# A hybrid decoder block on one core: the local half gated straight from PSUM during the latent steps

## The chip, the core and the metric

The kernel runs on one core of a Trainium2 chip. The core has five engines, each with an instruction queue of its own: PE (TensorE, matrix products into PSUM), DVE (VectorE), ACT (ScalarE), POOL (GpSimd) and SP (SyncE, which here issues DMAs). Each queue is worked off in order; semaphores tie the queues together. The metric is the device time of one execution in microseconds; the median of three runs is compared.

## What is computed

One block of a decoder for 1024 tokens of width 1024, in fp32: two kinds of attention side by side, each with its own output product and its own sigmoid gate, then an output product, a residual and a gated FFN.

```python
h    = rmsnorm(x, mix_norm_g)
qa, ka, va, q_lat, kv_lat, k_r, g_a, g_b = split(h @ w_in)
o_a  = swa_sink_attention(rope(qa), rope(ka), va, sinks)      # local: 8 heads of 64, window 128
o_b  = mla_attention(...)                                    # latent: 8 heads, causal over all 1024
y    = sigmoid(g_a) * (o_a @ w_o_swa) + sigmoid(g_b) * (o_b @ w_o_mla)
x    = x + y @ w_out
h    = rmsnorm(x, ffn_norm_g)
x    = x + (silu(h @ w_gate) * (h @ w_up)) @ w_down          # D_FF = 2816
return rmsnorm(x, final_norm_g)
```

What is below called the local half is `sigmoid(g_a) * (o_a @ w_o_swa)`.

## The kernel before

**Products.** Each operand is split into a high and a low part by `split` (line 160: ACT copies the high part, L163, DVE subtracts it from the source to get the low part, L166), and `mm3` (lines 172 to 174) makes three matmuls of them. One matmul has 512 columns; its output stands in a PSUM bank. The large products, the output product and the FFN go by a scheme with seven products instead of eight (`Seven`, `xo`), which needs sums and differences of operand blocks; additions and subtractions stand in the helpers `add` (L180) and `sub` (L177), which are given the engine to use.

**Stages**, in the profile's time: projections and the gate product (to 345 us), which leaves the gates' pre-activations `g_a` and `g_b` in DRAM as 16 tiles `gate_d[0..15]` of 128 columns of y by 1024 tokens, and the local attention; latent q, k and v (to 379); the latent steps (379 to 564); `mix_b` (564 to 608); the output product `xo` (608 to 690), which ends with the second RMSNorm; the FFN (690 to 1113) and its down product.

**The latent steps.** 64 steps t, 8 heads of 8 query blocks. A step issues the score matmuls of step t+2 (L1245 to 1247), then transposes its own probabilities `p` (L1272). For each block of scores DVE adds the mask and reduces (L1255, result `nmb`), ACT takes the exponential (L1256), POOL inverts the row sum and scales (L1257, 1258), PE transposes into `pTb`, and ACT and DVE split the transposed block (`pth`, `ptl`). PE has room between these for other products: the table `fill` puts a half of a local product `mix_a(dc, sh, c0, n)` into some of the steps. `dc` is one of 8 column blocks of y, `sh` a half of the tokens; each pair (dc, sh) has one PSUM tile `oA`, which is complete after the second half. `mix_a` then copies oA into SBUF by ACT (L1351), and for dc ≥ 4 stores the result `ar` to DRAM. Thirteen of the 16 are in steps, three at or after the last step.

**mix_b.** For the 8 column blocks in the order `DCS = (0, 1, 4, 5, 2, 3, 6, 7)`, `load_sigs` loads the two gate tiles (and `ar` where it was stored), `sigmoids` applies the sigmoid on ACT (L1328, one 128x1024 instruction a tile) and multiplies `ar` by the first gate on POOL (L1526, two halves). `mix_b` makes the latent product `oB`, multiplies it by the second gate on DVE out of PSUM (L1503), and adds or subtracts the two halves; the result y then stands where the first gate was (`ya`). Sums of y's row blocks, which the output product needs, are made by DMAs that accumulate (`left_sum`, issued by POOL): by the table `SUMS` five inside mix_b, and eleven after it.

**The sums of w_out.** `out_sums(i)` makes sums of blocks of w_out in DRAM, in seven parts. Part 0 (two copies of 1 MB on SP's queue) is issued in the second step of the local attention, the parts 1 to 6 in the latent steps 40 to 58 by `OUT_AT`.

**The end of the output product.** `xo(q, b)` makes product q for row block b and adds it into `x2` or subtracts it (DVE, out of PSUM). `norm_a(b)` squares on ACT and gets ms and rstd on POOL (L360, L363); `norm_b(b)` scales on DVE (L1742); `to_h` transposes into the FFN's operand (L1575). From here to the FFN's 15th product PE, DVE, ACT and POOL follow the order in which the code is written (`manual_schedule`). Into it are put the loads of the first FFN weights (`ffn.load_part`, L1619) and the sums of their blocks (`ffn.mix(0)`, six POOL instructions, L180 and L177).

**The FFN.** For 11 block pairs j the gate and up products run through `Seven.run` (`fa`, `fb` in PSUM; `wl` the split weights; `pu` a partial result). `wd_out(j)` loads two tiles of w_down, makes four differences on POOL (L177, `wd`), and stores them for the down product: for j = 0 and 1 in their own blocks, where it follows product 5; for the rest after product 2 of their block; the last one too in block 3.

Of the kernel before, what the change touches and what calls it, by code (L numbers as in the profile page):

```python
# [89 lines left out]
def hybrid_block_kernel(  # L90
# [989 lines left out]
    for it in range(N_SW):  # L1080
# [6 lines left out]
        if it == 1:  # L1087
            out_sums(0)
# [238 lines left out]
    def sigmoid(i):  # L1327
        a = nc.scalar.activation(gate[i], gate[i], AF.Sigmoid)  # L1328
        if held[0]:
            tc.keep_in_program_order(a)  # L1330
# [4 lines left out]
    def mix_a(dc, sh, c0, n, ps=None):  # L1335
# [3 lines left out]
        if (sh, c0) == (0, 0):  # L1339
            if dc >= 4:  # L1340
                ar[dc] = U("ar")
# [8 lines left out]
        if c0 + n == 4:  # L1350
            nc.scalar.copy(ar[dc][:, half(sh)], oa_ps.pop((dc, sh)))  # L1351
            if sh == 1 and dc >= 4:
                nc.sync.dma_start(ar_d[dc - 4], ar.pop(dc))
# [16 lines left out]
    DCS = (0, 1, 4, 5, 2, 3, 6, 7)  # L1370

    def load_sigs(dc):
        for i in (dc, 8 + dc):
            load_sig(i)
# [42 lines left out]
    w_at = {t: u[0] // 2 for t, u in fill.items() if u[0] % 2 == 0 and u[1:] == (0, 0)}  # L1417
    pvq = []
    OUT_AT = {40: 1, 43: 2, 47: 3, 50: 4, 54: 5, 58: 6}
    for t in range(NT):  # L1420
# [25 lines left out]
        held[0] = True  # L1446
        if t == 3:
            load_oa(0, 1)
            load_oa(1, 1)
# [16 lines left out]
    if LATE:  # L1466
        mix_a(*rest.pop(0), 0, 4, PX("oA"))
    for _, hp, j in pvq:
        pv(hp, j)
    if not LATE:  # L1470
        mix_a(*rest.pop(0), 0, 4, PX("oA"))
# [7 lines left out]
    def mix_b(dc, i):  # L1479
# [3 lines left out]
        ga, gb = gate.pop(dc), gate.pop(8 + dc)  # L1483
        ya[dc] = ga

        def mixed(sh):
            cs = half(sh)
            if dc < 4:
                add(ga[:, cs], ga[:, cs], gb[:, cs], nc.vector)
            else:  # L1490
                nc.vector.scalar_tensor_tensor(ga[:, cs], ga[:, cs], -1.0, gb[:, cs], op0=ALU.mult, op1=ALU.subtract)

        def mixed_split(sh):
            cs = half(sh)
            if dc >= 4 or sh == 0:
                hi, lo = left[1 if dc < 4 else 2 if sh == 0 else 4]
                split(hi[:, dc % 4], lo[:, dc % 4], ga[:, cs])

        for sh in range(2):
# [3 lines left out]
            nc.vector.tensor_tensor(gb[:, cs], pb, gb[:, cs], op=ALU.mult)  # L1503
# [17 lines left out]
    def sigmoids(dc):  # L1521
        for i in (dc, 8 + dc):
            sigmoid(i)
        a_ = ar.pop(dc)
        for sh in range(2):
            nc.gpsimd.tensor_tensor(gate[dc][:, half(sh)], a_[:, half(sh)], gate[dc][:, half(sh)], op=ALU.mult)  # L1526

# [4 lines left out]
    sigmoids(DCS[0])  # L1532
# [3 lines left out]
    SUMS = {6: [(0, 0), (0, 1)], 7: [(0, 2), (1, 0), (1, 1)]}  # L1536
# [3 lines left out]
    for i, dc in enumerate(DCS):  # L1540
        if i in (1, 2):
            st.load_to(st.index[("ob", (1, 3)[i - 1])])
# [6 lines left out]
        if i + 1 < 8:  # L1549
            sigmoids(DCS[i + 1])  # L1550
        for n, k in SUMS.get(i, ()):
            left_sum(n, k)
        if i == 2:
# [3 lines left out]
        if i in (1, 3):  # L1557
# [529 lines left out]
```

## Time and profile before

| | us |
|---|---|
| runs | 1334.76, 1332.06, 1332.71 |
| median | 1332.71 |
| profiled execution | 1334.28 |
| its span | 1332.5 |

The median is what a later time is compared with; durations below come from the profiled execution, whose span is from the first instruction to the last. The clock that was granted to TensorE was 0.999 of full speed over the span.

How to read the rows shown in the prediction: a row of the timeline holds the start in us from the begin of the span, the duration in us, the engine, the line of the kernel, the operation, `out<-in`, the shapes, the count, and in brackets the idle time before it with what ended it. A row of the groups holds the count, then the busy time and the mean ns of one, then the idle time before them. An idle engine costs nothing unless another one waits for it.

### The profile page before, as it was taken

To read this page: it belongs to the slowest core of one execution; us is meant where nothing else is said; L and a number is where in the kernel's file an instruction comes from. 1 tells how busy PE (TensorE), PEld (TensorE's weight loads), DVE (VectorE), ACT (ScalarE), POOL (GpSimd) and SP (SyncE) were. 2 spreads that over 40 slices of the span, in tenths; PEclk is the share of its full clock that TensorE was granted. 3 is DMA by queue.
4 is the path that set the end of the run, shared out by engine and by line. 5 is a ranking of instruction groups with operands and counts; after the bars stand their busy time and mean duration, and the time that the engine had idled before them with its cause. 6 is when DMAs were issued, how large, how long until landed. Compare 5 with 4: busy or idle time off the path is not lost. (4 is left out here: it accounts for less than half of the span.)

```text
span 1332.5 us, 19056 instructions
## 1 busy us (share of the span) xinstructions
PE 1316.1 (99%) x6516; PEld 1105.5 (83%) x6516; DVE 923.7 (69%) x1493; ACT 644.4 (48%) x1306; POOL 592.7 (44%) x638
## 2 busy tenths in 40 slices
PE   9999999999999999999999999999999999999997
PEld 6899888888888888887887788888888888888886
DVE  7868677776767766698779766665665564663862
ACT  7434667665547666764555322323233222644452
POOL 2116546643324556354242765755676531022521
PEclk9999999999999999999999999999999999999999
DMA  9454532344476446879822354534543425996504
GB/s 375 156 185 156 170 116 84 100 135 171 169 227 184 96 111 143 271 298 244 240 109 101 142 189 166 207 136 171 182 167 141 167 100 194 365 379 241 174 17 141
DMA packets 89121, 237.26 MB, mean 178 GB/s; under 512 B 10049, under 2 KB 16705, under 8 KB 87873
## 3 DMA queue, kind: packets, MB, share of 16 engines
q1 hardware_dynamic: 84192, 225.29, 49.0%
q0 software_dynamic: 3392, 8.39, 3.5%
q10 hardware_dynamic: 1440, 2.36, 0.5%
q8 instruction: 52, 0.85, 0.3%
q14 instruction: 45, 0.36, 0.1%
HBM read 161.16 MB, written 78.51 MB: 180 GB/s over the span
## 5 line engine op out<-in xcount | busy, mean ns | idle before, releaser
L166 DVE TENSOR_TENSOR wl<-wr,wl 128x512 fp32r<-128x512 f32 x150 | 149.4, 1019 | 73.8 <-ACT wl L163 73.3
L166 DVE TENSOR_TENSOR lrv<-lr,lrv 128x1024 fp32r<-128x1024 f32 x77 | 105.1, 1396 | 50.2 <-ACT lrv L163 44.6
L163 ACT CAST lrv<-lr 128x1024 fp32r<-128x1024 f32 x77 | 80.1, 1052 | 95.0 <-PE fd L174 55.4
L172 PE MATMUL fd<-lrv 128*128 128x512 f32 x308 | 119.9, 389 | 0.0
L174 PE MATMUL fd<-lrv 128*128 128x512 f32 x308 | 119.8, 389 | 0.0
L173 PE MATMUL fd<-lrv 128*128 128x512 f32 x308 | 119.8, 389 | 0.0
L177 POOL TENSOR_TENSOR wr<-wr,sm 128x512 f32<-128x512 f32 (+1 forms) x38 | 45.7, 1211 | 147.9 <-DVE wl L166 129.6
L163 ACT CAST wl<-wr 128x512 fp32r<-128x512 f32 x150 | 87.3, 622 | 6.2 <-DVE t3l L177 2.8
L1257 POOL TENSOR_TENSOR denb<-denb,neg_one 128x1 f32<-128x1 f32 x64 | 40.8, 643 | 91.8 <-ACT p L1256 80.0
L166 DVE TENSOR_TENSOR wl<-sm,wl 128x512 fp32r<-128x512 f32 x60 | 51.7, 885 | 43.1 <-ACT wl L163 43.0
L173 PEld LDWEIGHTS fd<-lrv 128*128 128x128 f32 x308 | 57.8, 188 | 12.1
L172 PEld LDWEIGHTS fd<-lrv 128*128 128x128 f32 x308 | 57.8, 188 | 12.1
L174 PEld LDWEIGHTS fd<-lrv 128*128 128x128 f32 x308 | 57.8, 188 | 11.9
L1256 ACT ACTIVATE p<-scb,nmb 128x384 f32<-128x384 f32 (+3 forms) x64 | 47.8, 747 | 33.4 <-DVE nmb L1255 24.6
L166 DVE TENSOR_TENSOR ptl<-pTb,pth 128x512 fp32r<-128x512 f32 (+2 forms) x96 | 50.5, 552 | 16.8 <-ACT pth L163 16.5
L1255 DVE CUSTOM_DVE_ANT_0 scb<-scb,mask 128x384 f32<-128x384 f32 (+3 forms) x64 | 48.6, 761 | 15.3 <-PE scb L1247 14.3
L360 POOL TENSOR_SCALAR ms<-ss 128x1 f32<-128x1 f32 x32 | 9.1, 286 | 111.7 <-ACT x L465 36.5
L1630 ACT ACTIVATE act<-sm 128x512 f32<-128x512 f32 x11 | 7.0, 633 | 99.7 <-DVE sm L180 99.7
L1258 POOL TENSOR_SCALAR p<-p,denb 128x384 f32<-128x384 f32 (+3 forms) x64 | 48.2, 758 | 6.1
L1630 ACT ACTIVATE act<-pu 128x512 f32<-128x512 f32 x22 | 13.9, 632 | 74.7 <-DVE pu L180 74.7
L172 PE MATMUL fb<-t3h,wl 128*128 128x512 f32 x120 | 47.4, 395 | 1.1 <-DVE pu L180 1.1
L172 PE MATMUL fa<-t1h,wl 128*128 128x512 f32 x120 | 47.2, 393 | 1.2 <-ACT wl L163 1.2
(355 smaller groups left out, 4340.7 us busy)
## 6 DMA issues: line engine op xcount, KB each, us to landing
lr<-la_d SPq DMA_DIRECT2D x77, 256.0 KB, 5.3
wr<-in_w_gate_dram SPq DMA_DIRECT2D x22, 512.0 KB, 4.3
wr<-in_w_up_dram SPq DMA_DIRECT2D x22, 512.0 KB, 5.1
wd<-in_w_down_dram SPq DMA_DIRECT2D x22, 512.0 KB, 7.1
rb_d<-wd SPq DMA_DIRECT2D x22, 512.0 KB, 2.7
la_d<-sd SPq DMA_DIRECT2D x22, 512.0 KB, 5.1
lr<-rb_d SPq DMA_DIRECT2D x44, 256.0 KB, 5.4
lr<-in_w_down_dram SPq DMA_DIRECT2D x33, 256.0 KB, 5.2
```

What stands on the lines that cost most here:

```text
L163: i = nc.scalar.copy(hi, src)
L166: (eng or nc.vector).tensor_tensor(lo, src, hi.bitcast(F32), op=ALU.subtract)
L172: nc.tensor.matmul(ps, ah, bh, start=first and i == 0, stop=False, skip_group_check=go_on)
L173: nc.tensor.matmul(ps, ah, bl, start=False, stop=False, skip_group_check=go_on)
L174: nc.tensor.matmul(ps, al, bh, start=False, stop=last and i == n - 1, skip_group_check=go_on)
L177: eng.tensor_tensor(out, a, b, op=ALU.subtract)
L360: nc.gpsimd.tensor_scalar(ms, ss, 1.0 / width, EPS, op0=ALU.mult, op1=ALU.add)
L1255: nc.vector.tensor_tensor_reduce(s_, s_, m_, 1.0, -NEG, op0=ALU.add, op1=ALU.min, accum_out=nm)
L1256: nc.scalar.activation(p_, s_, AF.Exp, scale=-1.0, bias=nm, accum_out=den)
L1257: nc.gpsimd.tensor_tensor(den, den, neg_one[:, 0:1], op=ALU.pow)
L1258: nc.gpsimd.tensor_scalar(p[:, 0:w], p[:, 0:w], den, 0.0, op0=ALU.mult, op1=ALU.add)
L1630: nc.scalar.activation(dst, src, AF.Silu)
```

## The change

The logistic function is written as sigmoid(x) = (1 + tanh(x/2))/2. ACT makes the tanh (`twice_sigmoid`), the factor 1 is added where the gate is multiplied, and the factor 1/2 stands in the output product's residual additions. In `mix_a`, DVE multiplies oA by the gate straight out of PSUM, so the first eight gates are loaded and activated during the latent steps, and neither an ACT copy nor the POOL multiplication remains. mix_b goes through the columns in pairs (0, 4), (1, 5), ..., the row sums stand between them, and the weights of oB come a column earlier. Part 0 of `out_sums` is in latent step 34. `ffn.mix(0)` is split in two (`mix_of`), each after another norm, and `wd_out(0)` and `wd_out(1)` are in FFN blocks 4 and 5.

```diff
         sw[it].pop("norm")()
-        if it == 1:
-            out_sums(0)
...
-    def sigmoid(i):
-        a = nc.scalar.activation(gate[i], gate[i], AF.Sigmoid)
+    def twice_sigmoid(g):
+        a = nc.scalar.activation(g, g, AF.Tanh, scale=0.5)
...
             if dc >= 4:
-                ar[dc] = U("ar")
+                ar[dc] = gate[dc]
...
         if c0 + n == 4:
-            nc.scalar.copy(ar[dc][:, half(sh)], oa_ps.pop((dc, sh)))
-            if sh == 1 and dc >= 4:
-                nc.sync.dma_start(ar_d[dc - 4], ar.pop(dc))
+            nc.vector.scalar_tensor_tensor(ar[dc][:, half(sh)], gate[dc][:, half(sh)], 1.0, oa_ps.pop((dc, sh)),
+                                           op0=ALU.add, op1=ALU.mult)
+            if sh == 1:
+                gate.pop(dc)
+                if dc >= 4:
+                    nc.sync.dma_start(ar_d[dc - 4], ar.pop(dc))
...
-    DCS = (0, 1, 4, 5, 2, 3, 6, 7)
+    DCS = (0, 4, 1, 5, 2, 6, 3, 7)
     def load_sigs(dc):
-        for i in (dc, 8 + dc):
-            load_sig(i)
+        load_sig(8 + dc)
...
+    g_at = {a: fill[b][0] for a, b in zip([3] + slots, slots) if fill[b][1:] == (0, 0)}
+    g_at[NT - 3] = 3
-    OUT_AT = {40: 1, 43: 2, 47: 3, 50: 4, 54: 5, 58: 6}
+    OUT_AT = {34: 0, 40: 1, 43: 2, 47: 3, 50: 4, 54: 5, 58: 6}
...
         held[0] = True
+        if t in g_at:
+            load_sig(g_at[t])
+        if t in fill and fill[t][1:] == (0, 0):
+            twice_sigmoid(gate[fill[t][0]])
+        if t == NT - 1:
+            twice_sigmoid(gate[3])
...
-        ga, gb = gate.pop(dc), gate.pop(8 + dc)
-        ya[dc] = ga
+        ga, gb = ar.pop(dc), gate.pop(8 + dc)
+        ya[dc] = gb
...
-            nc.vector.tensor_tensor(gb[:, cs], pb, gb[:, cs], op=ALU.mult)
+            nc.vector.scalar_tensor_tensor(gb[:, cs], gb[:, cs], 1.0, pb, op0=ALU.add, op1=ALU.mult)
...
-    def sigmoids(dc):
-        for i in (dc, 8 + dc):
-            sigmoid(i)
-        a_ = ar.pop(dc)
-        for sh in range(2):
-            nc.gpsimd.tensor_tensor(gate[dc][:, half(sh)], a_[:, half(sh)], gate[dc][:, half(sh)], op=ALU.mult)
...
-    SUMS = {6: [(0, 0), (0, 1)], 7: [(0, 2), (1, 0), (1, 1)]}
+    SUMS = {2: [(0, 0)], 3: [(1, 0)], 4: [(0, 1), (2, 0)], 5: [(1, 1), (3, 0)], 6: [(0, 2), (2, 1)], 7: [(1, 2), (3, 1)]}
...
-        if i in (1, 2):
-            st.load_to(st.index[("ob", (1, 3)[i - 1])])
+        if i in (0, 1):
+            st.load_to(st.index[("ob", (1, 3)[i])])
...
-            sigmoids(DCS[i + 1])
+            twice_sigmoid(gate[8 + DCS[i + 1]])
...
-        if i in (1, 3):
-            st.conv_to(st.index[("ob", (1, 3)[i // 2])])
+        if i in (1, 2):
+            st.conv_to(st.index[("ob", (1, 3)[i - 1])])
...
-        if q in (1, 5, 7):
-            add(x_, ps, x_, nc.vector)
-        else:
-            sub(x_, x_, ps, nc.vector)
+        nc.vector.scalar_tensor_tensor(x_, ps, 0.5 if q in (1, 5, 7) else -0.5, x_, op0=ALU.mult, op1=ALU.add)
...
+    def mix_of(m):
+        a11, a21, a22 = ffn.part(0, m, 0, 0), ffn.part(0, m, 0, 1), ffn.part(0, m, 1, 1)
+        t = ffn.sums[(0, m)] = U("sm", F32, (P, 2, 4, P))
+        add(t[:, 0], a21, a22, nc.gpsimd)
+        sub(t[:, 1], t[:, 0], a11, nc.gpsimd)
+        sub(a21, a11, a21, nc.gpsimd)
...
-    for n, k in ((0, 3), (1, 2), (2, 0), (2, 1), (1, 3), (2, 2), (3, 0), (3, 1), (2, 3), (3, 2), (3, 3)):
+    for n, k in ((0, 3), (2, 2), (1, 3), (3, 2), (2, 3), (3, 3)):
...
     norm_a(1)
+    mix_of("g")
...
     norm_a(2)
+    mix_of("u")
...
     norm_a(3)
-    ffn.mix(0)
...
-        if (q, m) == (5 if j < 2 else 2, "u"):
-            if j < HF - 1:
-                wd_out(j)
+        if (q, m) == (2, "u") and 2 <= j < HF - 1:
+            wd_out(j)
+        if (q, m) == (4, "u") and j in (4, 5):
+            wd_out(j - 4)
```

`ffn.load_part(0, 0)` and `ffn.load_part(0, 1)` each stand one product of `xo` earlier than before.

Three places in the order of rows, where a row holds the line, the operation and `out<-in` with the tiles' names (the numbers behind names tell tiles of one kind apart). The first is on DVE, in latent steps around step 33, before and then after the change:

```order
L1255 ISA scb_5525,nmb_5532<-scb_5525,mask_4054 128x1024
L1255 ISA nmb_5532 128x1
L166 TENSOR_TENSOR ptl_5518<-pTb_5519,pth_5517 128x3x128
L1255 ISA scb_5553,nmb_5557<-scb_5553,mask_4054 128x128
L1255 ISA nmb_5557 128x1
L166 TENSOR_TENSOR ptl_5518<-pTb_5546,pth_5517 128x4x128
```

```order
L1253 ISA scb_5531,nmb_5538<-scb_5531,mask_4052 128x1024
L1253 ISA nmb_5538 128x1
L166 TENSOR_TENSOR ptl_5524<-pTb_5525,pth_5523 128x3x128
L1349 SCALAR_TENSOR_TENSOR sg_5425<-sg_5425,oA_5458 128x512
L1253 ISA scb_5559,nmb_5563<-scb_5559,mask_4052 128x128
L1253 ISA nmb_5563 128x1
L166 TENSOR_TENSOR ptl_5524<-pTb_5552,pth_5523 128x4x128
```

The product with oA (L1349) stands between a split and the next reduction (L1255 before, L1253 after). On ACT, at the same place, before and after:

```order
L163 CAST pth_5462<-pTb_5493 128x2x128
L1256 ACTIVATE p_5480,denb_5481<-scb_5475,nmb_5479 128x512
L1256 ACTIVATE p_5506,denb_5507<-scb_5498,nmb_5505 128x896
L163 CAST pth_5517<-pTb_5519 128x3x128
L1256 ACTIVATE p_5533,denb_5534<-scb_5525,nmb_5532 128x1024
L1351 COPY ar_5453<-oA_5452 128x512
L163 CAST pth_5517<-pTb_5546 128x4x128
```

```order
L163 CAST pth_5467<-pTb_5499 128x2x128
L1326 ACTIVATE sg_5425<-sg_5425 128x1024
L1254 ACTIVATE p_5486,denb_5487<-scb_5481,nmb_5485 128x512
L1254 ACTIVATE p_5512,denb_5513<-scb_5504,nmb_5511 128x896
L163 CAST pth_5523<-pTb_5525 128x3x128
L1254 ACTIVATE p_5539,denb_5540<-scb_5531,nmb_5538 128x1024
L163 CAST pth_5523<-pTb_5552 128x4x128
```

The copy of oA (L1351) is gone, and a tanh of a whole gate tile (L1326) stands ahead of two exponentials. The third place is on POOL, at the end of the output product: `ms` and `rstd` are those of norms 3 and 4 before, and of norms 1, 2 and 3 after:

```order
L360 TENSOR_SCALAR ms_7491<-ss_7489 128x1
L363 TENSOR_TENSOR rstd_7493<-ms_7491,neg_half 128x1
L180 TENSOR_TENSOR sm_7495<-wr_7348,wr_7377 128x512
L177 TENSOR_TENSOR sm_7495<-sm_7495,wr_7348 128x512
L177 TENSOR_TENSOR wr_7348<-wr_7348 128x4x128
L180 TENSOR_TENSOR sm_7499<-wr_7349,wr_7378 128x512
L177 TENSOR_TENSOR sm_7499<-sm_7499,wr_7349 128x512
L177 TENSOR_TENSOR wr_7349<-wr_7349 128x4x128
L360 TENSOR_SCALAR ms_7554<-ss_7552 128x1
L363 TENSOR_TENSOR rstd_7556<-ms_7554,neg_half 128x1
```

```order
L360 TENSOR_SCALAR ms_7355<-ss_7353 128x1
L363 TENSOR_TENSOR rstd_7357<-ms_7355,neg_half 128x1
L180 TENSOR_TENSOR sm_7359<-wr_7285,wr_7314 128x512
L177 TENSOR_TENSOR sm_7359<-sm_7359,wr_7285 128x512
L177 TENSOR_TENSOR wr_7285<-wr_7285 128x4x128
L360 TENSOR_SCALAR ms_7417<-ss_7415 128x1
L363 TENSOR_TENSOR rstd_7419<-ms_7417,neg_half 128x1
L180 TENSOR_TENSOR sm_7421<-wr_7286,wr_7315 128x512
L177 TENSOR_TENSOR sm_7421<-sm_7421,wr_7286 128x512
L177 TENSOR_TENSOR wr_7286<-wr_7286 128x4x128
L360 TENSOR_SCALAR ms_7479<-ss_7477 128x1
L363 TENSOR_TENSOR rstd_7481<-ms_7479,neg_half 128x1
```

The six instructions that stood in one block between norms 3 and 4 stand in two blocks of three, between norms 1 and 2 and between norms 2 and 3.

19 lines of the change are left out of this document (8 added, 11 removed).

## The prediction, made before the change had run

> **What bounds the kernel now.** I read the busy line first, then windows by stage, then what TensorE waited for, then the rows around each wait.
>
> ```profile
> PE 1316.1 (99%) x6516; PEld 1105.5 (83%) x6516; DVE 923.7 (69%) x1493; ACT 644.4 (48%) x1306; POOL 592.7 (44%) x638
> 379.00:564.00 185.00, 182.30 (x1147) 160.00 (x1146) 132.12 (x275) 127.38 (x289) 91.38 (x132) 1.00 0.59 164
> 564.00:608.00 44.00, 43.90 (x192) 35.46 (x191) 37.95 (x40) 28.58 (x34) 25.39 (x16) 1.00 0.78 287
> 608.00:690.00 82.00, 81.43 (x376) 66.57 (x375) 63.33 (x83) 39.43 (x65) 28.79 (x35) 1.00 0.72 203
> 690.00:751.00 61.00, 58.78 (x267) 47.49 (x265) 57.94 (x80) 31.18 (x58) 21.64 (x17) 1.00 0.33 119
> 751.00:1113.00 362.00, 361.85 (x1596) 299.66 (x1597) 226.67 (x268) 105.42 (x189) 219.13 (x152) 1.00 0.46 163
> ```
>
> A windows row holds the stretch, its length, the busy time of PE, PEld, DVE, ACT and POOL, the granted clock, the DMA share and GB/s. The five stretches are the latent steps, mix_b, the output product, the head of the FFN, and the rest of the FFN. TensorE is busy everywhere, so only its gaps can be won. The fourth stretch differs: DVE is at 57.94 of 61 us, so there DVE sets the pace. The waits of PE name the gaps, first from 564 to 760, then in the latent steps (engine and line, who was waited for, total, times, longest):
>
> ```profile
> PE fb L172 <- DVE pu L180: 1.1, 1, 1.1
> PE fa L172 <- ACT pu L861: 0.7, 1, 0.7
> PE tp L1575 <- DVE xn L1742: 0.5, 1, 0.5
> PE xo L172 <- ACT yh L163: 0.3, 1, 0.3
> PE xo L173 <- DVE wv L166: 0.2, 1, 0.2
> ...
> PE scb L1245 <- ACT p L1256: 1.1, 3, 0.6
> 700.87 0.39 PE L173 MATMUL fa<-b21l,wl 128*128 128x512 f32 x1
> 701.10 0.39 PE L174 MATMUL fa<-b21h,wl 128*128 128x512 f32 x1
> 702.22 0.50 PE L172 MATMUL fa<-b21h,wl 128*128 128x512 f32 x1 [0.73 <-ACT pu L861]
> ```
>
> The last three rows show what a gap costs. Matmuls of 512 columns start every 0.23 us (700.87, 701.10) and are drawn 0.39 long, so an idle of 0.73 is a start 1.12 after the last, 0.89 lost: every idle hides 0.16 more. The three gaps at the FFN's head, with that, lose 1.1+0.16, 0.7+0.16 (0.89) and 0.5+0.16: some 2.8 us.
>
> **The FFN's head: −2.8 us.** Two edits take POOL work away from it.
>
> ```profile
> 673.12 1.51 POOL L180 TENSOR_TENSOR sm<-wr,wr 128x512 f32<-128x512 f32 x1
> ...
> 682.91 0.19 POOL L360 TENSOR_SCALAR ms<-ss 128x1 f32<-128x1 f32 x1
> 678.56 0.19 ACT L1737 ACTIVATION_READ_ACCUMULATOR xn<-x 128x1 f32 x1
> 683.77 1.28 DVE L1742 SCALAR_TENSOR_TENSOR xn<-x,rstd,ffng 128x1024 f32<-128x1024 f32 x1 [1.49 <-POOL rstd L363]
> ```
>
> First, `ffn.mix(0)`, six operations from 673.12 until shortly before 682.91, stands on POOL ahead of the ms and rstd of norm 4. Its sum of squares was there at 678.75, but ms ran at 682.91, and DVE idled 1.49 us for it. DVE is the pacing engine here, so those 1.49 reach the next two gaps of PE, 0.66 and 0.89. Now three operations follow norm 1's rstd and three norm 2's; norm 4's rstd, done about 0.9 after its ms starts (682.91, and the waiting xn at 683.77), would come at about 679.7, before DVE is free (683.77 − 1.49 = 682.28). I take −1.5.
>
> ```profile
> 734.42 3.48 DVE L166 TENSOR_TENSOR wl<-wr,wl 128x512 fp32r<-128x512 f32 x2
> 735.61 1.74 POOL L177 TENSOR_TENSOR wd<-wd 128x512 f32<-128x512 f32 x1
> 741.23 1.77 DVE L166 TENSOR_TENSOR wl<-sm,wl 128x512 fp32r<-128x512 f32 x1
> 743.52 0.68 DVE L166 TENSOR_TENSOR wl<-sm,wl 128x512 fp32r<-128x512 f32 x1
> ```
>
> Second, `wd_out(0)` runs on POOL at 735 to 742. DVE subtractions beside it take 1.74 to 1.77 us, the same ones alone 0.68: three of them lose 2×1.06 + 1.09 = 3.2 us, and the gap of 1.26 that waits for DVE `pu` comes 8 us later. Without it I take −1.3. Together −2.8; bounds 0 (DVE stays late for its other 58 us of work) and −3.5 (smaller gaps go too). By the Trainium skill, "SBUF — State Buffer", Who interferes with whom, a DVE instruction with two SBUF inputs contends with a GpSimd one that reads SBUF, exclusively; by that rule, the trace agrees (1.77 against 0.68), and the whole 3.2 comes back.
>
> The two blocks go to FFN blocks 4 and 5. There nothing waits: PE 361.85 of 362 with DVE at 226.67 (63%) through all of the FFN blocks that hold the nine other calls, one of them two. Price 0; if the cover were gone, 3.2 us per call.
>
> **mix_b and the output product: −1.0 us.** POOL's 16 multiplications go, DVE's product with oB becomes one instruction that adds 1 and multiplies, and eleven row sums ahead of the output product become six, with ten instead of five inside mix_b.
>
> ```profile
> L1526 POOL TENSOR_TENSOR sg<-ar,sg 128x512 f32<-128x512 f32 x16 | 26.2, 1658 | 28.6 <-ACT sg L1328 28.6
> L1503 DVE TENSOR_TENSOR sg<-oB,sg 128x512 f32<-128x512 f32 x16 | 10.9, 681 | 2.5 <-ACT sg L1328 2.5
> L1189 DVE SCALAR_TENSOR_TENSOR qns<-q,qns 128x512 fp32r<-128x512 f32 x6 | 4.0, 686 | 3.2 <-ACT qns L1188 3.2
> L180 DVE TENSOR_TENSOR sg<-sg,sg 128x512 f32<-128x512 f32 x8 | 9.3, 1165 | 0.5
> ```
>
> The two-operation form with one PSUM input takes 686 ns against 681: 32 of them, in mix_b and the output product, cost 0.2 us of DVE, which had 6 and 19 us free. The eight additions L180 (1165 ns, beside those POOL rows) should near 0.7: DVE gains up to 3.9 us. So the output product's operand `yh` and the weights `wv` should be ready: their gaps, 0.3+0.16 and 0.2+0.16, are worth 0.8, and small ones make it 1.0. Bounds 0 and −1.5. The added sums are DMAs in the stretch with the highest share, 0.78; they leave the one after (0.72) by as many. The order in pairs (0, 4, 1, 5, ...) has every pair's rows complete two columns after they start, which is what lets a sum start at the third column; it adds no instruction, and the weights of oB are loaded and split one column earlier.
>
> **The latent steps: +0.5 us.** The 16 ACT copies of oA become DVE instructions, 13 of them inside the steps, and 8 tanh (half of the 16 gate activations, each of the same 128x1024) join ACT there.
>
> ```profile
> L1351 ACT COPY ar<-oA 128x512 f32<-128x512 f32 x16 | 9.3, 584 | 8.0 <-PE oA L174 7.9
> L1328 ACT ACTIVATE sg<-sg 128x1024 f32<-128x1024 f32 x16 | 16.3, 1053 | 0.0
> L1255 DVE CUSTOM_DVE_ANT_0 scb<-scb,mask 128x384 f32<-128x384 f32 (+3 forms) x64 | 48.6, 761 | 15.3 <-PE scb L1247 14.3
> ACT p L1256 <- DVE nmb L1255: 22.8, 26, 1.9
> 467.32 0.40 PE L174 MATMUL oA<-wv,wv 128*128 128x512 f32 x1
> 468.13 0.33 PE L1247 MATMUL scb<-kT,qT 96*128 96x384 f32 x1
> ```
>
> ACT: 8×1.05 − 13×0.584 = +0.8 us, and the 7.9 us in which it stood before a copy until oA was ready are gone, and nothing on ACT gets later by it. DVE: 13×0.69 = +9.0 us on 132 of 185, at the head of a queue whose next entry is mostly a score reduction. The chain that can hurt: the reduction gives `nmb`, ACT's exp waits for it (22.8 us in 26 waits), and PE waits for exp (1.1 in 3). But the reduction itself waits 14.3 us for PE's scores: DVE is ahead of PE. In the order of rows nearly every product with oA is followed by a reduction whose scores PE issues after that oA: here oA's last matmul starts at 467.32 and the last of the next scores at 468.13, 0.8 later, so 0.69 fits between them. Two of the 13 stand ahead of a split whose transposition PE ends first, and can hold it back by up to 0.7 each: 1.4 at most, with scores two steps ahead (a step is 185/64 = 2.9 us). On the other side PE's waits for exp, 1.1+3×0.16 = 1.6, may vanish because ACT no longer stands waiting for oA. New waits: a gate load is queued on SP behind the store of a product with oA (dc ≥ 4), which waits for DVE, and its tanh stands in ACT's order ahead of the next exps, which PE's transpositions wait for. Mostly three or four steps (9 to 12 us) lie between load and tanh, but from step 29 to 30 and from 57 to 58 one (2.9 us).
>
> ```profile
> oar<-oa_d SPq DMA_DIRECT2D x4, 512.0 KB, 5.6
> ```
>
> A load of that size in these steps lands after 5.6 us, so ACT may stand 5.6 − 2.9 = 2.7 us twice. The chain behind it (reduction 0.76, exp and POOL's two rows about as long each) fills some 3 of the 5.8 us of lead, so PE loses little of the 2.7: 0.25 a place. With the 1.4 set off against the 1.6 I take +0.5. Bounds +9.0 (all thirteen products exposed) and −1.6.
>
> A rule against this edit: the Trainium skill, "VectorE: DVE Perf Modes", Specifications, has VectorE sitting closer to SBUF and ScalarE closer to PSUM, so the evacuation moves to the engine that is worse at it. The rows agree as far as 584 against 686 ns go, and by them alone the move would cost 16×0.1 = 1.6 us of engine time, and the sum would be 1.6 higher if all of it were exposed.
>
> **The rest: 0.** `out_sums(0)` leaves its place at 154 us, on SP:
>
> ```profile
> 153.44 0.50 PE L172 MATMUL fa<-t1h,wl 128*128 128x512 f32 x1 [1.18 <-ACT wl L163]
> 154.27 1.23 SPq L337 DMA_DIRECT2D wt_d<-in_w_out_dram  x2
> ```
>
> The only wait that is listed for PE from 139 to 345 ends at 153.44, before those copies are issued; nothing there is won. At its new place, step 34, a further 2 MB on SP's queue lies in a stretch with a DMA share of 0.59; its first user is the sum at step 40, six steps later (6×2.9 = 17 us).
>
> Sum: −2.8 − 1.0 + 0.5 = −3.3. The profiled run took 1334.28, its span 1332.5, so the same run would take 1331.0. It lies 1.6 above the median of 1332.71; by the median 1329.4.
>
> **Rivals.**
>
> *DVE in the latent steps decides* (slower). DVE takes its rows in order, so each product with oA that waits for PE holds back the reduction and the transposition's split behind it. Place: the change's L1349 ahead of its L1253 (the reduction). With all 13 exposed 9.0 − 3.8 = +5.2: 1337.9. From 6 exposed the change no longer wins, from 10 it loses over 0.2%. For it: PE already waits for exp. Against: the reductions' 14.3 us of waiting. Chance 0.22.
>
> *The split mix holds up the norms* (same). Three operations stand ahead of norm 2's ms and may wait for weights.
>
> ```profile
> 655.10 0.48 SPq L1619 DMA_DIRECT2D wr<-in_w_up_dram  x1
> wr<-in_w_up_dram SPq DMA_DIRECT2D x22, 512.0 KB, 5.1
> 659.94 0.55 POOL L363 TENSOR_TENSOR rstd<-ms,neg_half 128x1 f32<-128x1 f32 x1
> 665.67 0.19 POOL L360 TENSOR_SCALAR ms<-ss 128x1 f32<-128x1 f32 x1 [5.19 <-ACT xn L1737]
> ```
>
> The gap from 660.5 to 665.67 is 5.2 and the operations take 4.9 (half of 673.12 to 682.91): it fits by 0.3, if weights are there. In the old place they land at 655.10+5.1 = 660.2, and one product earlier now. Late by 2 or 3 us, norm 2 and what follows it would give the head's 2.8 back: 1331.7; from 6.5 us on it turns slower than the 0.2% below. Chance 0.09.
>
> *The head stays DVE-bound* (same). With 57.94 of 61 us busy, each gap closed can open behind the next late row; only 1 us is kept over all: 1331.7. For it: DVE idles just 3 us there. Against: 4.7 us leave DVE's path. Chance 0.13.
>
> *The steps gain too.* ACT, rid of 7.9 us of waiting, brings exp forward, and of the lost time there 3 us go, twice the waits for exp: 1329.4 − 3.0 = 1326.4. For it: PE's first wait there is for ACT `p`. Against: most of the 2.7 us by which PE's 182.30 misses 185 has other causes. Chance 0.10.
>
> The forecast keeps 0.46. 0.2% is 2.7 us, about what a measurement of this kernel can tell from no change: faster means below 1330.0. The forecast lies 0.6 beyond that, and its own range is 1326.5 to 1331.5: 0.30 of its 0.46 go to faster, 0.16 to same. With the steps' gain, 0.10, and 0.06 of the two rivals that end near no change, faster is 0.46. Slower is 0.20: 0.17 of the first rival (10 and more exposed) and 0.03 of the split mix. Same is the rest, 0.34. The range runs from 1325.0 to 1336.5: the steps' gain at its low end, all but full exposure of the thirteen at its high one.
>
> **What would show it.** Right: in the new profile no PE wait for `xn`, `pu` at the head, norm 4's rstd not behind any POOL add, DVE rows of 0.7 where 1.7 stood at 734 to 742, L1349 at some 0.69 us with reductions still waiting for PE scores. Wrong: PE waits for `p` or `scb` in the latent steps above 2 us, exp waiting for `nmb` well over 22.8 us, or new waits on DVE at the head; then the forecast falls by that term.

## The result and the profile after

The changed kernel takes 1328.81 us (median of 6 runs, 1326.63 to 1329.56); the kernel before, on the same chip, 1333.03 (1332.06 to 1334.76). The ratio is 0.9962, with a 95% interval of 0.9952 to 0.9972: 5.1 us faster, between 3.7 and 6.4. It is not the ratio of the two medians, which lie 4.2 us apart. Forecast were 3.3 us faster and 1329.4.

The busy line of the page after the change, and two stretches of its windows view (stretch, length, busy time of PE, PEld, DVE, ACT, POOL, granted clock, DMA share, GB/s):

```profile
PE 1315.0 (99%) x6516; PEld 1107.4 (83%) x6516; DVE 916.1 (69%) x1509; ACT 635.8 (48%) x1289; POOL 563.6 (42%) x622
```

```profile
608.00:690.00 82.00, 82.00 (x384) 68.28 (x383) 62.00 (x80) 36.80 (x62) 21.04 (x27) 1.00 0.55 167
690.00:751.00 61.00, 61.00 (x281) 50.44 (x280) 55.33 (x79) 28.88 (x54) 22.06 (x17) 1.00 0.26 93
```

PE has no idle time left in the output product and at the FFN's head, where it was busy 81.43 of 82 and 58.78 of 61. The view of PE's waits from 564 to 760, which had five rows before, has none. Such windows are cut at fixed times, though; where a kernel starts later, its work lies elsewhere in them. So I measure the stages between the starts of their first matmuls, which the timeline gives, in us:

| kernel | to the first scores | latent steps | mix_b | output product | FFN | down product | span |
|---|---|---|---|---|---|---|---|
| before | 379.48 | 184.12 | 44.40 | 82.20 | 425.54 | 216.76 | 1332.5 |
| after | 378.95 | 185.23 | 43.52 | 80.48 | 422.14 | 216.66 | 1327.0 |

(The output product runs to its last matmul, the FFN from there to the first of the down product.) The terms of the change stand in the four columns in the middle: +1.1 in the latent steps, −0.9 in mix_b, −1.7 in the output product, −3.4 in the FFN, together −4.9, which agrees with the −5.1 of the runs. The first column differs by 0.5; it differs by up to 5 us between executions of kernels that are alike there (376.4 to 381.2 in the runs below), so it is start-up and no part of the change. Where the code of a stage is the same, the latent steps and mix_b repeat within 0.2 us and the FFN within 0.5; the output product of e1, with the code of before, took 0.5 more. So one profile can tell changes of 1 us apart which the runs, with an interval of some 1.3 us to each side, hardly do; a difference below 0.5 in the output product or the FFN counts only with a wait that shows it.

### The profile page after: what moved, and what is told of

It is laid out like the page before. It is cut to its first block, busy times and chain, and to the rows that moved or that the text cites. A ratio compares the mean times of both kernels' runs of the same rounds, so it can differ in the third digit from the quotient of the medians.

```text
span 1327.0 us, 19016 instructions
## 1 busy us (share of the span) xinstructions
PE 1315.0 (99%) x6516; PEld 1107.4 (83%) x6516; DVE 916.1 (69%) x1509; ACT 635.8 (48%) x1289; POOL 563.6 (42%) x622
## 4 chain that ended last, share of the span: by engine, by line
PE 62%; POOL 2%; issue 2%; DVE 1%; ACT 0%; POOLq 0%; DVEq 0%; ACTq 0%
PE fa L174 6%; PE fa L173 6%; PE fa L172 6%; PE fd L172 5%; PE fd L173 5%; PE fd L174 5%; PE fb L173 5%; PE fb L174 5%; PE fb L172 5%; PE xo L174 2%; PE xo L172 2%; PE xo L173 2%; POOL p L1256 1%; POOL denb L1255 1%; PE oB L173 1%
## 5 line engine op out<-in xcount | busy, mean ns | idle before, releaser
L166 DVE TENSOR_TENSOR wl<-wr,wl 128x512 fp32r<-128x512 f32 x150 | 144.3, 984 | 74.2 <-ACT wl L163 73.7
L1255 POOL TENSOR_TENSOR denb<-denb,neg_one 128x1 f32<-128x1 f32 x64 | 40.0, 624 | 92.5 <-ACT p L1254 80.5
L1253 DVE CUSTOM_DVE_ANT_0 scb<-scb,mask 128x384 f32<-128x384 f32 (+3 forms) x64 | 48.4, 760 | 17.1 <-PE scb L1245 15.6
L163 ACT CAST pth<-pTb 128x512 fp32r<-128x512 f32 (+2 forms) x96 | 43.4, 480 | 18.1 <-PE pTb L1270 17.2
L172 PE MATMUL fb<-t2h,wl 128*128 128x512 f32 x120 | 47.4, 395 | 0.0
```

Source lines behind the costliest of these rows:

```text
L163: i = nc.scalar.copy(hi, src)
L166: (eng or nc.vector).tensor_tensor(lo, src, hi.bitcast(F32), op=ALU.subtract)
L172: nc.tensor.matmul(ps, ah, bh, start=first and i == 0, stop=False, skip_group_check=go_on)
L1253: nc.vector.tensor_tensor_reduce(s_, s_, m_, 1.0, -NEG, op0=ALU.add, op1=ALU.min, accum_out=nm)
L1255: nc.gpsimd.tensor_tensor(den, den, neg_one[:, 0:1], op=ALU.pow)
```

## The experiments

Twelve kernels, all of them variants of before or after. The table holds the ratio to before with its interval (none for e6 and e7, which leave out a part of the computation and were timed only once) and the stages.

| run | edit | ratio | latent steps | mix_b | output product | FFN |
|---|---|---|---|---|---|---|
| e1 | before, `wd_out` moved | 0.9996 [0.9987, 1.0004] | 184.15 | 44.41 | 82.73 | 424.22 |
| e2 | before, mix split, loads earlier | 1.0014 [1.0005, 1.0024] | 184.15 | 44.42 | 86.49 | 424.23 |
| e3 | after, old list of sums | 0.9963 [0.9950, 0.9976] | 185.17 | 43.52 | 80.48 | 421.85 |
| e4 | after, `out_sums(0)` back | 0.9962 [0.9950, 0.9975] | 188.29 | 43.52 | 80.48 | 422.09 |
| e5 | after, second DVE instruction | 0.9981 [0.9971, 0.9992] | 188.73 | 43.52 | 80.45 | 421.84 |
| e6 | after, no tanh in the steps | – | 184.18 | 43.52 | 80.48 | 422.25 |
| e7 | after, ACT copies, no gating | – | 184.75 | 43.52 | 80.48 | 421.92 |
| e8 | after, sums held to the last tanh | 0.9960 [0.9946, 0.9974] | 185.25 | 43.52 | 80.48 | 421.91 |
| e9 | after, FFN's head as before | 0.9984 [0.9974, 0.9993] | 185.27 | 43.52 | 80.48 | 425.04 |
| e10 | after, sums held to mix_b's end | 0.9994 [0.9984, 1.0004] | 185.35 | 43.52 | 85.54 | 422.29 |
| b3 | after, tanh at short steps | 0.9964 [0.9952, 0.9977] | 185.12 | 43.52 | 80.48 | 421.91 |
| b4 | b3, weights split earlier | 0.9952 [0.9938, 0.9965] | 185.97 | 43.52 | 80.45 | 421.96 |

### The FFN's head: each edit alone, and both undone

e1 is the kernel before with one edit:

```diff
-        if (q, m) == (5 if j < 2 else 2, "u"):
-            if j < HF - 1:
-                wd_out(j)
+        if (q, m) == (2, "u") and 2 <= j < HF - 1:
+            wd_out(j)
+        if (q, m) == (4, "u") and j in (4, 5):
+            wd_out(j - 4)
```

> The kernel before with only wd_out(0) and wd_out(1) moved to FFN blocks 4 and 5. My theory: the subtractions on DVE at 734 to 742 us take 0.7 instead of 1.7 us, the wait of PE for pu at 749 us (1.1 idle, 1.28 lost) is gone, the other two gaps at the FFN's head stay: -1.3 us, and nothing is lost in blocks 4 and 5. Rival (the head stays DVE-bound): the gap reappears behind the next DVE row, 0 to -0.4 us.

PE's waits from 600 to 760 in e1:

```profile
PE fa L172 <- ACT pu L861: 0.7, 1, 0.7
PE tp L1575 <- DVE xn L1742: 0.5, 1, 0.5
PE xo L172 <- ACT yh L163: 0.5, 1, 0.5
PE xo L173 <- DVE wv L166: 0.2, 1, 0.2
```

The wait of `fb` for `pu` is gone and the other two of the head are there as before. e1's timelines of POOL and DVE show why; the first and the last of the DVE rows answer to 734.42 and 741.23 of before, the one between them to a row of 1.18 us at 738.42:

```profile
732.49 1.62 POOL L177 TENSOR_TENSOR wr<-wr,sm 128x512 f32<-128x512 f32 x1 [1.88 <-ACT act L1630]
732.88 2.38 DVE L166 TENSOR_TENSOR wl<-wr,wl 128x512 fp32r<-128x512 f32 x2
735.79 0.68 DVE L166 TENSOR_TENSOR wl<-wr,wl 128x512 fp32r<-128x512 f32 x1
736.99 0.68 DVE L166 TENSOR_TENSOR wl<-sm,wl 128x512 fp32r<-128x512 f32 x1
```

Of the pair only one subtraction got faster, 2.38 us for both instead of 3.48: the other stands beside a POOL row that isn't `wd_out`'s and stays. The next two went from 1.18 and 1.77 to 0.68, and the product `act` between them (L1632) from 1.78 to 0.68, 3.8 us in all. The FFN is 425.54 − 424.22 = 1.3 us shorter, blocks 4 and 5 included. The runs alone don't show it: the whole kernel is 0.5 us faster by the ratio, with an interval that holds nothing as well as the 0.8 by which the stages are shorter (the output product took 0.5 more here).

e2 is the kernel before with the other edit (the two loads also leave their old places, behind `norm_b(0)` and behind `norm_a(1)`; that is two products of `xo` earlier, not one as I wrote in the description of the change):

```diff
     ahead(4, 0)
+    ffn.load_part(0, 0)
     xo(3, 0)
...
     ahead(4, 1)
+    ffn.load_part(0, 1)
...
     norm_a(1)
+    mix_of("g")
...
     norm_a(2)
+    mix_of("u")
...
     norm_a(3)
-    ffn.mix(0)
```

> The kernel before with only ffn.mix(0) split in two behind norms 1 and 2, and its loads one product earlier. My theory: norm 4's DVE instruction no longer idles 1.49 us for rstd, the gaps of PE for xn and pu (0.64 and 0.89 lost) go: -1.5 us; the gap at 749 us stays. Rival (DVE-bound): 0 to -0.5. Rival (the split mix waits for weights and holds up norm 2): 0 to +2, with ms of norm 2 ended by a POOL add.

The FFN gained 1.3 us, as expected, but the output product lost 4.3, and the kernel is slower than before. e2's PE waits, then its timeline on POOL, SP and PE (the last row sum, the first FFN load, the gap), and the first two of these before the change:

```profile
PE xo L172 <- ACT yh L163: 2.2, 2, 2.0
PE fb L172 <- DVE pu L180: 1.1, 1, 1.1
PE tp L1575 <- DVE xn L1742: 0.8, 1, 0.8
PE fa L172 <- ACT pu L861: 0.3, 1, 0.3
PE xo L173 <- DVE wv L166: 0.2, 1, 0.2
```

```profile
641.67 0.88 POOL L328 DMA_DIRECT2D sg<-sg  x1 [1.84 <-DMA sg<-sg]
...
640.02 0.33 SPq L1619 DMA_DIRECT2D wr<-in_w_gate_dram  x1
...
650.57 0.50 PE L172 MATMUL xo<-wv,yh 128*128 128x512 f32 x1 [2.01 <-ACT yh L163]
```

```profile
643.71 0.88 POOL L328 DMA_DIRECT2D sg<-sg  x1 [1.86 <-DMA sg<-sg]
653.34 0.67 SPq L1619 DMA_DIRECT2D wr<-in_w_gate_dram  x1
```

Before, the FFN's first load was issued 10 us after the last row sum, because it stood behind the first store of x2; in e2 it is issued 1.7 us ahead of it. The last three row sums, with KB each and us from issue to landing, before (639 to 650 us) and in e2 (637 to 650), where the first FFN loads run beside them:

```profile
sg<-sg POOLq DMA_DIRECT2D x3, 256.0 KB, 4.1
```

```profile
sg<-sg POOLq DMA_DIRECT2D x3, 256.0 KB, 7.7
```

The sums land later, the split of `yh` behind them is late, and PE waits 2.0. No mix operation has run by then, so of the two parts of the edit it is the loads. The wait for `xn` in the list is not the one of the FFN's head, which is gone: it stands inside the output product, at 673.46, and what makes it these runs don't settle. Of the wait for `pu` at the head 0.3 of 0.7 is left. POOL's `ms` rows in e2 still wait for ACT, not for a mix operation (668.32, ended by ACT `xn`), so it isn't the wait for weights of my rival.

e9 undoes both edits in the changed kernel (the diffs of e1 and e2 the other way round).

> The changed kernel with the head of the FFN as before: ffn.mix(0) in one piece behind norm 3, the loads one product later, wd_out(0) and (1) in their own blocks. If the head's two edits gained 3.4 us there and need nothing else: the stretch from the last product of xo to the down product 425.5 us again, the output product 80.5: +3.4. If the gated local half alone made part of it (DVE less behind): +2.

```profile
PE fb L172 <- DVE pu L180: 1.1, 1, 1.1
PE fa L172 <- ACT pu L861: 0.7, 1, 0.7
```

Two of the three waits are back, and the FFN is 2.9 us longer; the third, for `xn`, isn't, so 0.5 us of the 3.4 came from the other parts of the change. The runs agree: 0.9984 against 0.9962 is 2.9 us. Together, then, the head's edits gain 2.9 where the row sums are early, and e1's and e2's gains in the FFN add up to 2.6.

### Where the output product's gain is from

In e3 the table of sums and the list behind mix_b are the old ones.

```diff
-    SUMS = {2: [(0, 0)], 3: [(1, 0)], 4: [(0, 1), (2, 0)], 5: [(1, 1), (3, 0)], 6: [(0, 2), (2, 1)], 7: [(1, 2), (3, 1)]}
+    SUMS = {6: [(0, 0), (0, 1)], 7: [(0, 2), (1, 0), (1, 1)]}
...
-    for n, k in ((0, 3), (2, 2), (1, 3), (3, 2), (2, 3), (3, 3)):
+    for n, k in ((0, 3), (1, 2), (2, 0), (2, 1), (1, 3), (2, 2), (3, 0), (3, 1), (2, 3), (3, 2), (3, 3)):
```

> The changed kernel with the row sums where they were: five inside mix_b, eleven after it. The trace of the change gained 0.9 us in mix_b and 1.7 in the output product, 2.6 where I had forecast 1.0. If the earlier sums are what made the output product's operands ready: +1.0 to +1.7 us in the output product, with PE waits for yh back. If it was the POOL multiplications that went: 0 to +0.3.

Nothing changed: 80.48. POOL has nothing but the sums to do in mix_b now, so a place further back in the code is no place further back in its queue; only the order among the sums differs. Before, the multiplications for the last column were ahead of the first sum. The first sum and the first matmul of the output product, of before and then of after, and after's last sum and first FFN load:

```profile
608.70 1.84 POOL L328 DMA_DIRECT2D sg<-sg  x2
608.00 0.39 PE L172 MATMUL xo<-wv,yh 128*128 128x512 f32 x1
```

```profile
578.41 0.94 POOL L328 DMA_DIRECT2D sg<-sg  x1 [24.30 <-DMA ffng<-in_ffn_g_dram]
607.70 0.39 PE L172 MATMUL xo<-wv,yh 128*128 128x512 f32 x1
627.32 0.88 POOL L328 DMA_DIRECT2D sg<-sg  x1 [4.14 <-DMA sg<-sg]
634.30 0.33 SPq L1617 DMA_DIRECT2D wr<-in_w_gate_dram  x1
```

The first sum moved from 0.7 us behind the output product's start to 29.3 ahead of it, and the last from 35.7 us behind it to 19.6. To test that this is the cause, e8 and e10 hold the sums back in the changed kernel by one tiny instruction ahead of them on POOL.

```diff
+        if i == 6:
+            g = gate[8 + DCS[7]][:, 0:1]
+            nc.gpsimd.tensor_scalar(g, g, 1.0, 0.0, op0=ALU.mult, op1=ALU.add)
         for n, k in SUMS.get(i, ()):
             left_sum(n, k)
```

(with e3's lists)

> The changed kernel with the sums in the old order (five, then eleven) and one instruction of 128x1 on POOL ahead of them that needs the last tanh, so that POOL issues the first sum when mix_b ends, as it did before behind the last of its multiplications. If the output product's gain came from POOL being free for the sums (first sum at 28 us ahead of the output product's start instead of 0.7 us after it): PE waits for yh come back, and, with the FFN's first weights now loaded earlier, more than the 1.7 us is lost there: +2 to +6 us. If the gain came from elsewhere: 0.

e8 missed its aim. The last tanh now comes 18 us before the output product starts, so the first sum was held only to there; the last came 27.2 us behind the start, as in e3, and the output product took 80.48. That sets a bound: a last sum at 27 us is in time, though the FFN's first load was issued 0.6 us ahead of it. e10 holds them to the end of mix_b:

```diff
+    g = ya[DCS[7]][:, 0:1]
+    nc.gpsimd.tensor_scalar(g, g, 1.0, 0.0, op0=ALU.mult, op1=ALU.add)
+    for n, k in ((0, 0), (0, 1), (0, 2), (1, 0), (1, 1)):
+        left_sum(n, k)
     pool_order.__exit__(None, None, None)
```

(the table empty, the old eleven behind it)

> The changed kernel with all row sums behind one instruction of 128x1 on POOL that needs the last column of y, in the old order, so the first sum is issued when mix_b ends. Holding them until the last tanh (17 us ahead of that) moved the last sum from 20 to 28 us behind the output product's start and cost nothing. If the output product's gain is POOL being free for the sums early: the last sum now comes at some 35 us as before, behind the FFN's first loads, PE waits for yh come back, and the output product takes 82.2 to 86 us where the change has 80.5. If not: 80.5.

e10's timeline on POOL and SP (the holding instruction, the first and the last sum, the first FFN load), and its PE waits from 600 to 760:

```profile
607.95 0.19 POOL L1560 TENSOR_SCALAR sg<-sg 128x1 f32<-128x1 f32 x1 [54.08 <-DVE yl L166]
608.43 0.94 POOL L328 DMA_DIRECT2D sg<-sg  x1 [0.29 <-issue]
642.78 0.88 POOL L328 DMA_DIRECT2D sg<-sg  x1 [2.28 <-DMA sg<-sg]
640.68 0.33 SPq L1621 DMA_DIRECT2D wr<-in_w_gate_dram  x1
```

```profile
PE xo L172 <- ACT yh L163: 2.1, 2, 1.6
```

One instruction of 0.19 us that holds the sums costs 85.54 − 80.48 = 5.1 us; the runs say 0.9994 against 0.9962, 4.3 us. Not all of it is waiting. Behind the gap of 1.6 us, which ends at 650.92, the granted clock (the third figure from the end in e10's windows) fell, and the matmuls started 0.43 us apart instead of 0.23 up to 654; compared with what follows e2's gap, that is some 1.3 of the 5.1 us.

```profile
650.00:652.00 2.00, 1.08 (x3) 0.84 (x4) 1.10 (x2) 1.75 (x3) 0.00 (x0) 0.74 0.00 0
652.00:654.00 2.00, 2.00 (x6) 1.58 (x5) 2.00 (x4) 1.29 (x2) 0.00 (x0) 0.50 0.00 0
```

So late sums make PE wait for `yh`. They are not the whole of the gain, though. I compared the start of each matmul of `xo`, counted from the first, with the same one of the changed kernel. Before is 0.86 us late behind two waits for `wv`, at 619 and 621, and a further 0.85 behind the wait for `yh` at 644. e1 and e2 have the first 0.86 too; e10, whose sums are as late as theirs, doesn't. What is late at 619 is DVE. The first split of `wv` in the output product and the matmul that waits for it before, and the same split in e10:

```profile
618.22 1.22 DVE L166 TENSOR_TENSOR wv<-wr,wv 128x1024 fp32r<-128x1024 f32 x1
619.49 0.50 PE L173 MATMUL xo<-wv,yh 128*128 128x512 f32 x1 [0.22 <-DVE wv L166]
```

```profile
611.01 1.22 DVE L166 TENSOR_TENSOR wv<-wr,wv 128x1024 fp32r<-128x1024 f32 x1
```

DVE's last rows of mix_b end 9.7 us behind the start of the output product before, and 3.0 behind it in e10. mix_b's own 0.9 points the same way: PE's weight loads for `oB` waited 1.2 us for DVE's L1503 before and don't wait for it in the changed kernel nor in e10. So of the 2.6 us in these two stages 0.85 is the sums, shown by e10, and 1.7 is DVE being ready sooner. Which edit frees DVE, the multiplications that went, the order of the columns or the earlier weights, no run separates. For the multiplications speak DVE's rows of the same shape, which take less time without them. The eight additions of the forecast are, after the change:

```profile
L180 DVE TENSOR_TENSOR sg<-ar,sg 128x512 f32<-128x512 f32 x8 | 5.5, 689 | 0.2
```

They took 1165 ns before; from 564 to 608 us the five splits of `wv` went from 1872 to 1220 ns and those of `yl` from 948 to 690.

The prices of the sums, then, without DVE's part: late sums with late loads (before) cost 0.85; late sums with early loads 5.1 in e10 (3.7 without the fall of the clock) and 3.9 in e2, where the gap for `xn` costs 1.2 more; early sums with early loads nothing.

### The latent steps

e5 puts another DVE instruction ahead of each of the 13 products with oA in the steps.

```diff
         if c0 + n == 4:
+            if n == 2:
+                nc.vector.tensor_scalar(oa_ps[(dc, sh)], oa_ps[(dc, sh)], 1.0, 0.0, op0=ALU.mult, op1=ALU.add)
             nc.vector.scalar_tensor_tensor(ar[dc][:, half(sh)], gate[dc][:, half(sh)], 1.0, oa_ps.pop((dc, sh)),
```

> The changed kernel with a second DVE instruction of the same size (oA times 1 in place) ahead of each of the 13 products with oA in the latent steps, so 26 instructions of some 0.7 us where there were 13. If the slower forecast's mechanism counts (DVE products stand in the way of score reductions), the latent steps get longer by as much per instruction as they did by the first 13: the trace gave +1.1 us for 13, so +1.1 to +9. If they lie in DVE's slack, as I had it: 0 to +0.5.

The 13 took 696 ns each, and the steps got 3.5 us longer: 0.27 each, 39% of their time. (The scheduler also places some matmuls in another order, so this holds for the instructions with their new order.) e6 and e7 take one of the two new kinds of work away:

```diff
-        if t in fill and fill[t][1:] == (0, 0):
-            twice_sigmoid(gate[fill[t][0]])
-        if t == NT - 1:
-            twice_sigmoid(gate[3])
```

> The changed kernel without the 8 tanh of the local gates in the latent steps (the gates are loaded and used as they are, so y is not the reference's); DVE's products stay. The latent steps took 185.2 us with the change and 184.1 before. If the tanh on ACT, held in order ahead of the exps, cost the 1.1 us: 184.1 here. If DVE's products did: 185.2.

```diff
-            nc.vector.scalar_tensor_tensor(ar[dc][:, half(sh)], gate[dc][:, half(sh)], 1.0, oa_ps.pop((dc, sh)),
-                                           op0=ALU.add, op1=ALU.mult)
+            nc.scalar.copy(ar[dc][:, half(sh)], oa_ps.pop((dc, sh)))
```

> The changed kernel with the local half copied out of PSUM by ACT again and not gated at all (gates are still loaded and activated in the steps; y is not the reference's): 16 DVE products gone, 16 ACT copies back. If DVE's products cost the 1.1 us of the latent steps: 184.1 here. If the tanh did, with the copies beside them: 185.2 to 186.

Without the tanh the steps take 184.18, what they took before; with the copies on ACT again they take 184.75. So the eight tanh cost 1.05 us and the exchange of ACT copies for DVE products 0.5, not independent of each other (e7 also leaves out the gating). The place where it is seen best, ACT's rows around step 30 after the change:

```profile
473.67 0.97 ACT L163 CAST pth<-pTb 128x512 fp32r<-128x512 f32 x2 [0.49 <-PE pTb L1270]
474.54 1.06 ACT L1326 ACTIVATE sg<-sg 128x1024 f32<-128x1024 f32 x1
475.50 0.68 ACT L1254 ACTIVATE p<-scb,nmb 128x512 f32<-128x512 f32 x1
```

The tanh has no idle time ahead of it, so its gate is there; but it takes 1 us of ACT ahead of the exp, and PE's next scores wait for that exp: against e6, 0.6 of the 1.05 us is lost at this one place. Before, ACT loads a table (1.28 us at 563.5) ahead of the first sigmoid; the changed kernel has no such row there or in the steps, though its tanh stand between exponentials. b3 and b4 try to do better: all tanh at steps whose next scores are short, and the splits of the local operands, and in b4 of the weights, a step earlier.

```diff
+    s_at = {NB * i + 5: i ^ 4 for i in range(8)}
+    g_at = {t - 3: i for t, i in s_at.items()}
...
-        if t < 4 or 6 <= t < 10:
+        if t < 4 or 5 <= t < 9:
...
+        if t in s_at:
+            twice_sigmoid(gate[s_at[t]])
```

> The changed kernel with all eight local tanh at the steps 5, 13, ..., 61 (where the next blocks of scores are short), the gates loaded three steps ahead, and the second half of the local operand split one step earlier. Without the tanh the latent steps took 184.2 us, with them 185.2. If it is the place of the tanh ahead of long exps that costs: 183.5 to 184.3, -1 to -1.5 us. If a tanh costs ACT the same everywhere: 185.

```diff
-        if t + 2 in w_at:
-            st.conv_to(st.index[("oa", w_at[t + 2])])
+        if t + 3 in w_at:
+            st.conv_to(st.index[("oa", w_at[t + 3])])
```

> As b3, and the weights of the local product split three steps ahead of their use instead of two. PE's waits for wv (0.5 lost at the last of these) go: -0.5 us against b3, 183 to 183.8 in the latent steps. If the split only pushes the exps behind it on ACT: 184 to 185.

Both miss. b3 has the steps at 185.12 and b4 at 185.97; gaps that go in one place come back in others. b4's ratio is the lowest of all, but its interval holds the ratio of the change, and its latent steps are longer, so it is not shown to be better. No version that beats the change was found.

### The copies of w_out

```diff
         sw[it].pop("norm")()
+        if it == 1:
+            out_sums(0)
...
-    OUT_AT = {34: 0, 40: 1, 43: 2, 47: 3, 50: 4, 54: 5, 58: 6}
+    OUT_AT = {40: 1, 43: 2, 47: 3, 50: 4, 54: 5, 58: 6}
```

> The changed kernel with part 0 of out_sums back in the local attention. My theory: 0. Rival (its two copies on SP delay what is queued behind them, or the load of w_in's gate columns): the PE wait of 1.2 at 152 us, which the trace of the change doesn't have, is back, +1.4 us; or the latent steps win up to 0.5 us since 2 MB less is moved in them.

The ratio is that of the change. PE's wait of 1.2 at 152 us isn't there, nor is it in e1 and e2, which have the copies in that place too: it belonged to the one execution that was profiled. But e4's profile has the latent steps at 188.29, 3.1 longer. e4's timeline on ACT and PE, where the changed kernel has the three rows above, and its windows behind it:

```profile
475.07 1.06 ACT L1328 ACTIVATE sg<-sg 128x1024 f32<-128x1024 f32 x1 [1.43 <-DMA sg<-gate_d]
...
476.84 0.50 PE L1245 MATMUL scb<-kT,qT 96*128 96x512 f32 x1 [1.61 <-ACT p L1256]
```

```profile
478.00:480.00 2.00, 2.00 (x7) 1.56 (x6) 1.23 (x3) 0.15 (x1) 1.74 (x3) 0.56 0.12 43
480.00:484.00 4.00, 4.00 (x25) 3.57 (x25) 2.10 (x7) 2.77 (x6) 2.36 (x4) 0.79 0.00 0
```

Here the tanh waits 1.43 us for its gate. The DMA views of e4 (455 to 490 us) and of the changed kernel (469 to 476), with KB each and us from issue to landing:

```profile
sg<-gate_d SPq DMA_DIRECT2D x1, 512.0 KB, 6.9
qT<-qn_d SPq DMA_DIRECT2D x1, 512.0 KB, 8.8
```

```profile
sg<-gate_d SPq DMA_DIRECT2D x1, 512.0 KB, 4.7
qT<-qn_d SPq DMA_DIRECT2D x1, 512.0 KB, 12.3
```

In the changed kernel the copies of w_out stand on SP between the gate load and the loads of `qT`; the gate lands sooner there and `qT`, for which nothing waits, later. So at this place the copies seem to shield a gate load that is issued only one step ahead: in none of the other profiles with the copies in the steps does a tanh wait for its gate, but only e4 was profiled without them. e4's runs don't show 3 us more, and the profiled one is the slowest of its eight, so the wait can't stand in most of its executions; how often it comes, I did not measure.

## Why the prediction was right, step by step

- **What bounds the kernel:** right. Only gaps of PE were won, and those at the FFN's head and in the output product are gone.
- **What a gap costs:** counted too low. I added 0.16 to each idle time. But the matmuls behind a gap start 0.34 and 0.39 apart for a few more, which I left out: the idle 0.28 at 644 cost 0.85, and the three gaps at the head 3.4 where I had 2.8. That makes up part of what the gain is larger than forecast.
- **The FFN's head, −2.8 us:** −3.4 in the traces, of which 2.9 are the two edits (e9). `wd_out`: forecast −1.3, e1 −1.3. The 3.2 us of DVE behind that forecast were near the 3.8 measured by luck: I counted a subtraction that another POOL row slows, and left out two that `wd_out` slows. The mix ahead of norm 4: forecast −1.5, e2 −1.3 within the FFN, where a part of the gap for `pu` stays. That the head stays DVE-bound is refuted: DVE's busy time there fell from 57.94 to 55.33 of 61, and no gap reopened.
- **The price of the split mix:** a step that failed, though the sum hid it. I had its loads "one product earlier" at no cost and feared only that POOL might wait for weights. They stand two products earlier, and ahead of a store of x2 for which SP's queue had waited, so they are issued 19 us earlier (634.30 against 653.34). With the sums where they were that costs 4.3 us in the output product (e2), more than the head gives. It is free in the change only since the sums are early. The parts don't add up, and I had added them.
- **mix_b and the output product, −1.0 us:** the term that was sized too small; −0.9 and −1.7 were measured, 2.6. I counted the listed waits for `yh` and `wv`, and no gap in mix_b. DVE gaining time, the cause I named, fits 1.7 of the 2.6, and its additions did fall from 1165 to 689 ns; that the multiplications are what frees it is argued from such rows, not tested alone. The shift of five sums into mix_b, which I counted with it, is worth nothing (e3). What counts for the other 0.85 is that POOL's queue has nothing ahead of the sums (e10), and I did not see that the last column's multiplications had held all of them back to 608.70.
- **The latent steps, +0.5 us:** +1.1. The value was near, the working not. I had the tanh's price in waiting for a gate load, and in the profile of the change no tanh waits; where it does, it costs 3 us and not 0.25 (e4). I wrote that nothing on ACT gets later; the tanh's own 1.06 us ahead of the exps is what costs (e6). The products on DVE, 0.5, are mostly in the slack that the reductions' waiting for PE had shown: they took 685 ns and the reductions still wait 15.6 us for scores (14.3 before). PE's waits for exp fell from 1.1 to 0.5, less than I hoped for.
- **The slower rival**, DVE's products ahead of the score reductions, is refuted at its price: 0.5 us for 13 and not 9.0. But its mechanism is there: 13 more cost 3.5 (e5). The slack was nearly used up.
- **The rival by which the steps gain too** didn't come: ACT no longer waits for oA, but it waits 17.2 us for PE's transposed blocks in place of 8.3.
- **The rest, 0:** right for the copies at 154 us (e4). They are not quite idle at their new place.

The Trainium skill's rule in "SBUF — State Buffer", Who interferes with whom, by which a DVE instruction with two SBUF inputs contends with one of GpSimd that reads SBUF, agrees with both places: 1165 ns with the multiplications beside it and 689 without, 1.77 us with `wd_out` beside it and 0.68 without. The rule in "VectorE: DVE Perf Modes", Specifications, by which VectorE sits closer to SBUF and ScalarE closer to PSUM, agrees with the rows, 685 ns against 584; whether any of the 0.5 us of e7 comes from that difference, no run separates.

## What to carry to other kernels

Ask of each operation in an in-order queue what stands behind it: PE never waited for the multiplications on POOL, but they held back the DMAs issued behind them. Two edits of one change may need each other: measure each alone before adding their gains. Price a gap from start to start, up to the matmul where the usual spacing is back. And where an engine looks idle enough, double the new work once; it tells how much slack is left.

## What the hardware showed that I had not expected

After e4's gap of 1.61 us the granted clock fell to 0.56 for two and 0.79 for the next four us, and matmuls of 512 columns started every 0.43 us instead of 0.23 (478.42 and 478.85 below), which doubles the price of that gap: at its end PE is 1.5 us later than in the changed kernel, and 3.1 us later at the end of the steps. e10 shows it once more, 0.74 and 0.50 behind a gap of 1.6 us. After the longer gap of e2, 2.01 us, at nearly the same place as e10's, the windows show a clock of 1.00. The Trainium skill, "TensorE: Matmul & The Clock Gate", Part 1: The HAM clock gate, has the clock halved after an idle window of some 3.4 us, with windows that run freely; none of the three gaps is that long, so the traces do not agree on the length, and why two of them lowered the clock and the longest not, these runs don't settle. e4's timeline on PE:

```profile
477.41 0.40 PE L1247 MATMUL scb<-kT,qT 96*128 96x512 f32 x1
477.65 0.39 PE L1245 MATMUL scb<-kT,qT 96*128 96x512 f32 x1
...
478.42 0.63 PE L173 MATMUL oA<-wv,wv 128*128 128x512 f32 x1
478.85 0.63 PE L174 MATMUL oA<-wv,wv 128*128 128x512 f32 x1
```
